# Seven block products instead of eight in both SwiGLUs of the last layer of a two-layer hybrid transformer

## The chip, the core and the metric

The kernel runs on one core of a Trainium2 chip. The core has a matrix engine (TensorE, "PE" in the rows, with its weight loads as "PEld"), a vector engine (DVE), an activation engine (ScalarE, "ACT"), GpSimd ("POOL") and a sync engine (SyncE, "SP") that issues the loads. Each engine runs its own instructions in order and waits on semaphores for the others. What counts is the device time of one execution, in microseconds (us).

## What is computed

Two layers work on 512 latent tokens and 256 context tokens of width 1024. Each layer is a SwiGLU half-step, a mixing block and a second SwiGLU half-step. The part that matters:

```python
def swiglu(x, w1, w3, w2):
    return (jax.nn.silu(x @ w1) * (x @ w3)) @ w2

def macaron_half(h, m, i, g, w1, w3, w2):
    y = swiglu(modulate(rms_norm(h, g), m[:, 3 * i], m[:, 3 * i + 1]), w1, w3, w2)
    return h + 0.5 * m[:, 3 * i + 2, None, :] * y
```

The hidden width is 2816. In the last layer the first SwiGLU runs on both streams (768 columns), the second on the latent tokens alone (512 columns).

## The kernel before

Activations lie transposed: 8 tiles `h[k]` of 128 features by 768 tokens, context in columns 0 to 255 and latents in 256 to 767. The normed input n exists as a high part `nhi` and a low part `nlo`, whose sum is the float32 value. Every product is three matmuls in `mm3` (L395 high by high, L396 high weight by low input, L397 low weight by high input). Weights are loaded in blocks of 128 by 1024 (`unit`, L387) into one of 3 `raw` buffers and split into one of 4 `w` tiles: ACT rounds to the high part (L402) and DVE subtracts it (L403).

`ffn` walks over 22 tiles f of 128 hidden features. `st1(f)` multiplies by w1 and w3: per weight 8 input tiles k, three matmuls each, on the 512 latent columns and on the 256 context columns, into the two big PSUM tiles S of two banks each. `evac` makes the gated value: silu on ACT (L638), the product on DVE (L639), its high part on ACT (L640), its low part on DVE (L641). Per pair of tiles `st2` multiplies by w2: 8 output tiles d, two f each, into one of 4 one-bank PSUM tiles B; DVE adds the result to h (L682). I call these the down products, or downs.

The first pair of tiles is made while the norm before it still delivers its operands. The norm (`norm_steps`) takes 1/rms from PSUM ("R") and then makes each tile: DVE scales h (`nt`, L594), ACT rounds it to `nhi` (L596), DVE subtracts for `nlo` (L599). One tile of a narrow norm goes to GpSimd. In the first SwiGLU of the last layer the latent columns come first and the context's after them; in the second the latents come in two halves of 256.

A list scheduler puts the instructions of each engine in order ahead of time, by the order of the program and by a model of the engines; what is said below of order is what it gave.

## Time and profile before

| | us |
|---|---|
| median of 3 runs | 2809.39 (2806.04 to 2809.98) |
| span of the profiled execution | 2808.0 |
| TensorE busy in it | 2741.3 (98%) |
| DVE busy | 1705.1 (61%) |
| ACT busy | 884.7 (32%) |
| last layer, first SwiGLU (768 columns) | about 1557 to 2122 |
| last layer, second SwiGLU (512 columns) | about 2431 to 2808 |

The profile is one execution. "Busy" of PE counts a matmul from its start to its modelled end, and neighbours overlap, so the duration of a matmul in a row (0.28 us for 256 columns) is longer than the distance from one start to the next (0.12 us). All costs of matmuls here are such distances. On DVE and ACT too the next instruction can start a little before the one ahead is done. The granted clock is the share of its full speed that TensorE was given.

### The profile page before, as it was taken

The page shows a single profiled execution, that of the slowest core. Times are in us where ns is not written, and L with a number is a line of the kernel's source. Part 1 is how long each engine was busy: PE and PEld are TensorE (multiplying, and loading weights), DVE is VectorE, ACT ScalarE, POOL GpSimd, SP SyncE. Part 2 cuts the span into 40 slices and gives each one's busy share as a digit, 9 for nine tenths or more (in the row PEclk, how much of TensorE's full clock was granted, in tenths as well). Part 3 has the DMA queues.
Part 4 walks back from the last instruction along what each step waited for, and adds up shares of the span by engine and source line. Part 5 has one row for each costly group of instructions (what it writes and reads, how often), then busy time and mean ns, then how long its engine had stood idle before and what let it go on. Part 6 is the DMA issues. An engine that isn't in the chain of part 4 may idle for free.

```text
span 2808.0 us, 38620 instructions
## 1 busy us (share of the span) xinstructions
PE 2741.3 (98%) x15548; PEld 2331.5 (83%) x15548; DVE 1705.1 (61%) x3071; ACT 884.7 (32%) x1553; POOL 287.3 (10%) x378
## 2 busy tenths in 40 slices
PE   6999999999899999999999999999999899999999
PEld 5788888889777788888888888888888777888887
DVE  8987767564875479986744644343446775454444
ACT  5311112133665441211211512112115665432221
POOL 5000000020442200000000200000001442100000
PEclk9999999999999999999999999999999999999999
DMA  6533334111200054454411212212111200133222
GB/s 227 173 122 128 129 104 141 63 57 55 79 1 16 19 173 143 164 166 130 156 60 61 64 58 68 68 46 76 61 60 53 77 22 23 39 113 96 92 98 75
DMA packets 78663, 249.50 MB, mean 89 GB/s; under 512 B 8978, under 2 KB 10642, under 8 KB 78484
## 3 DMA queue, kind: packets, MB, share of 16 engines
q1 hardware_dynamic: 78484, 247.03, 26.9%
q8 instruction: 122, 2.00, 0.3%
q14 instruction: 57, 0.47, 0.1%
HBM read 244.90 MB, written 2.10 MB: 88 GB/s over the span
## 4 chain that ended last, share of the span: by engine, by line
PE 91%; DVE 5%; ACT 2%; POOL 1%; issue 1%; DMA 0%; SPq 0%; DVEq 0%; ACTq 0%; POOLq 0%
PE S L396 17%; PE S L395 17%; PE S L397 17%; PE B L395 11%; PE B L396 11%; PE B L397 11%; PE B L1151 3%; PE B L1302 2%; PE B L1270 1%; DVE junk L482 1%; DVE w L403 0%; DVE nt L274 0%; PE B L543 0%; PE B L1195 0%; ACT P L1139 0%
## 5 line engine op out<-in xcount | busy, mean ns | idle before, releaser
L396 PE MATMUL S<-nlo,w 128*128 128x512 f32 (+1 forms) x2448 | 847.8, 347 | 6.6 <-DVE nlo L276 5.2
L395 PE MATMUL S<-nhi,w 128*128 128x512 f32 (+1 forms) x2448 | 837.7, 346 | 7.1 <-ACT nhi L596 3.0
L397 PE MATMUL S<-nhi,w 128*128 128x512 f32 (+1 forms) x2448 | 843.5, 345 | 0.0
L402 ACT CAST w<-raw 128x1024 fp32r<-128x1024 f32 (+1 forms) x309 | 317.6, 1042 | 1178.9 <-issue 858.2
L682 DVE SCALAR_TENSOR_TENSOR h<-B,g,h 128x512 f32<-128x512 f32 (+1 forms) x616 | 376.4, 634 | 323.4 <-PE B L397 322.8
L396 PEld LDWEIGHTS S<-nlo,w 128*128 128x128 f32 x2448 | 462.0, 189 | 69.6 <-DVE nlo L276 7.4
L395 PEld LDWEIGHTS S<-nhi,w 128*128 128x128 f32 x2448 | 459.7, 189 | 67.9 <-ACT nhi L596 3.6
L397 PEld LDWEIGHTS S<-nhi,w 128*128 128x128 f32 x2448 | 462.3, 189 | 58.5
L403 DVE TENSOR_TENSOR w<-raw,w 128x1024 fp32r<-128x1024 f32 (+1 forms) x309 | 375.4, 1227 | 222.0 <-ACT w L402 219.8
L395 PE MATMUL B<-ghi,w 128*128 128x512 f32 (+1 forms) x1232 | 426.5, 348 | 0.0
L396 PE MATMUL B<-glo,w 128*128 128x512 f32 (+1 forms) x1232 | 425.9, 346 | 0.0
L397 PE MATMUL B<-ghi,w 128*128 128x512 f32 (+1 forms) x1232 | 425.1, 346 | 0.0
L482 DVE CUSTOM_DVE_ANT_0 junk<-ada,bc,mpart 128x768 f32<-128x768 f32 x238 | 244.5, 1027 | 41.6 <-DMA ada<-in_w_ada 36.4
L396 PEld LDWEIGHTS B<-glo,w 128*128 128x128 f32 x1232 | 232.4, 189 | 35.4 <-issue 1.3
L395 PEld LDWEIGHTS B<-ghi,w 128*128 128x128 f32 x1232 | 231.8, 189 | 35.9 <-DVE h L682 1.3
L397 PEld LDWEIGHTS B<-ghi,w 128*128 128x128 f32 x1232 | 232.3, 189 | 31.1
L639 DVE TENSOR_TENSOR silu<-silu,S 128x768 f32<-128x768 f32 (+2 forms) x89 | 75.3, 846 | 235.5 <-PE S L397 225.2
L531 POOL TENSOR_TENSOR sq<-sq,sq 128x512 f32<-128x512 f32 (+1 forms) x38 | 44.3, 1165 | 1642.0 <-ACT sq L527 1640.9
L638 ACT ACTIVATE silu<-S 128x768 f32<-128x768 f32 (+2 forms) x89 | 64.5, 725 | 316.4 <-PE S L397 315.8
L482 DVE CUSTOM_DVE_ANT_0 junk<-ada,bc,sml 128x256 f32<-128x256 f32 x238 | 119.2, 501 | 4.2
L1145 POOL TENSOR_SCALAR P<-P,rd 128x768 f32<-128x768 f32 (+3 forms) x120 | 97.6, 816 | 216.8 <-DVE rd L1144 203.2
L1134 DVE TENSOR_REDUCE nm<-S 128x1 f32<-128x768 f32 (+3 forms) x120 | 94.6, 792 | 37.6 <-PE S L397 28.9
(227 smaller groups left out, 3152.4 us busy)
## 6 DMA issues: line engine op xcount, KB each, us to landing
raw<-in_w SPq DMA_DIRECT2D x264, 512.0 KB, 3.6
ada<-in_w_ada SPq DMA_DIRECT2D x171, 384.0 KB, 4.1
raw<-in_w_out SPq DMA_DIRECT2D x16, 512.0 KB, 3.8
ada<-in_ada SPq DMA_DIRECT2D x16, 384.0 KB, 6.1
raw<-in_w_in_t SPq DMA_DIRECT2D x10, 512.0 KB, 3.3
raw<-in_dftx SPq DMA_DIRECT2D x8, 512.0 KB, 3.3
ada<-in_ada SPq DMA_DIRECT2D x8, 256.0 KB, 7.1
h<-in_hT SPq DMA_DIRECT2D x8, 256.0 KB, 5.8
```

Source lines behind the costliest of these rows:

```text
L395: mm(out, lhs[0], rhs[0], start=start, stop=False)
L396: mm(out, lhs[0], rhs[1], start=False, stop=False)
L397: mm(out, lhs[1], rhs[0], start=False, stop=stop)
L402: nc.scalar.copy(hi, src)
L403: nc.vector.tensor_sub(lo, src, hi.bitcast(F32))
L482: nc.vector.tensor_tensor_reduce(out=self.junk[:, 0:w.shape[1]], in0=w, in1=v, scale=1.0, scalar=init, op0=ALU.mult, op1=ALU.add, accum_ou ...
L638: self.last_silu = nc.scalar.activation(s, p1, AF.Silu)
L639: nc.vector.tensor_mul(s, s, p3)
L682: nc.vector.scalar_tensor_tensor(out=self.h[d][:, c0:c1], in0=ps[:, 0:c1 - c0], scalar=gate()[:, d, s:s + 1], in1=self.h[d][:, c0:c1], op0 ...
L1134: self.last_max = nc.vector.tensor_reduce(out=nm, in_=ps[:, c0:c1], axis=AX.X, op=ALU.max, negate=True)
L1145: nc.gpsimd.tensor_scalar(out=P, in0=P, scalar1=rd, scalar2=1.0, op0=ALU.mult, op1=ALU.mult)
L1151: mm(outs[y], lhs[y], rhs[y], start=start, stop=stop)
```

## The change

In the last layer `ffn7` takes the place of `ffn`. The input n is cut into two halves of its features (tiles 0 to 3 and 4 to 7) and two halves of its columns (`n1` and `n2`: 384 wide in the first SwiGLU, 256 in the second); the weights of a pair of f tiles are cut likewise, into four blocks of 512 inputs by one f tile of w1 and of w3. The first pair is made as before, in eight block products (`first_pair`). Each of the other 10 pairs is made in seven products, in the order B11, B21, E, t3, t1, t4, B22. A product is 2 by 4 by 3 matmuls, 24 in all, into one S tile, and the tiles keep running sums: before the next product is added, ACT copies the tile to SBUF (`snapshot`, 3 per pair), and a later result is PSUM plus a copy (`gated`: DVE adds, ACT takes silu, DVE multiplies; L883 to L885 of the new kernel).

The products need sums of weight blocks, 4 per pair on DVE (L967 to L971, 128 by 1024 each), so that 7 blocks are split per pair instead of 4, with w2's 2 as before. They need sums of the four quarters of n, made once per SwiGLU (`combine`, L834 to L837, 16 instructions) and split into 8 more operand pairs `cu` and `cv`. For that the norm ahead keeps its float32 tiles (`nf` instead of `nt`), finishes each in place on ACT (L610), and sends no tile to GpSimd. `raw` buffers go from 3 to 5, the 3 KB slots from 46 to 44. The downs of a pair follow B11 of the next one in the program. The rotary tables of the last layer are made after its first SwiGLU. The weights of w1 and w3 of the last layer are packed by blocks. The lines of the code behind the diff's first edits stand one or more lower in the new kernel (L403 becomes L404, L594 becomes L600, L599 becomes L605).

```diff
-    def __init__(self, b, l, shift, goff, ns, n=None):
+    def __init__(self, b, l, shift, goff, ns, n=None, keep=False):
         self.b, self.l, self.shift, self.goff, self.ns, self.n = b, l, shift, goff, ns, n
         self.acc, self.a = {}, None
+        self.t = {} if keep else None
-        pool = () if cols[1] - cols[0] == SEQ else (5,)
-        return self.b.norm_steps(self.acc, cols, self.n, self.l, self.shift, self.a, pool)
+        pool = () if cols[1] - cols[0] == SEQ or self.t is not None else (5,)
+        return self.b.norm_steps(self.acc, cols, self.n, self.l, self.shift, self.a, pool, self.t)
...
-    def __init__(self, nc, tc, aps, pools, slots=46, wslots=4, raws=3):
+    def __init__(self, nc, tc, aps, pools, slots=44, wslots=4, raws=5):
...
-            ts[k] = self.m3(w, base="nt")
+            if keep is None:
+                ts[k] = self.m3(w, base="nt")
+            else:
+                if k not in keep:
+                    keep[k] = self.m3(base="nf")
+                ts[k] = keep[k][:, c0:c1]
             nc.vector.scalar_tensor_tensor(out=ts[k], in0=self.h[k][:, c0:c1], scalar=a(k)[:, s:s + 1], in1=box["R"][:, 0:w],
                                            op0=ALU.mult, op1=ALU.mult)
             nc.scalar.activation(n[k][0][:, c0:c1], ts[k], AF.Identity, bias=shift(k))
...
         def rest(k):
             done[k] = nc.vector.scalar_tensor_tensor(out=n[k][1][:, c0:c1], in0=ts[k], scalar=shift(k),
                                                      in1=n[k][0][:, c0:c1].bitcast(F32), op0=ALU.add, op1=ALU.subtract)
-            self.free(ts.pop(k))
+            if keep is None:
+                self.free(ts.pop(k))
+            else:
+                nc.scalar.activation(ts[k], ts[k], AF.Identity, bias=shift(k))
...
+    def block(self, src):
+        r = self.mp.tile([128, 1024], F32, tag="raw", name=self.name("raw"), bufs=self.raws)
+        if src is not None:
+            self.nc.sync.dma_start(r, src)
+        return r
+    def split_block(self, r, scale=None):
+        w = self.mp.tile([128, 2, 1024], F32R, tag="w", name=self.name("w"), bufs=self.wslots)
+        self.split_psum(w[:, 0], w[:, 1], r, scale)
+        return w
...
+    def ffn7(self, l, i, n, t, gate, nxt, streams=(X_COLS, C_COLS), split=None, late=None):
...
+        mp13, w2 = self.a["w13s"][i], self.a["w2"][l, i]
+        x_only = len(streams) == 1
+        halves = X_HALVES if x_only else ((0, T // 2), (T // 2, T))
+        wd = halves[0][1] - halves[0][0]
+        n1, n2 = (slice(*c) for c in halves)
+        off = {X_COLS: 512, C_COLS: 256}
+        np_ = NF // 2
...
+        def combine(k):
+            u, v = t.pop(k), t.pop(k + 4)
+            tensor = nc.vector.tensor_tensor
+            tensor(out=u[:, n1], in0=u[:, n1], in1=u[:, n2], op=ALU.subtract)
+            tensor(out=u[:, n2], in0=v[:, n2], in1=u[:, n2], op=ALU.subtract)
+            tensor(out=v[:, n2], in0=u[:, n1], in1=v[:, n2], op=ALU.add)
+            tensor(out=v[:, n1], in0=v[:, n2], in1=v[:, n1], op=ALU.subtract)
+            c = slice(halves[0][0], halves[1][1])
+            for x, name in ((u, "u"), (v, "v")):
+                hi, lo = self.hl(T, "c" + name)
+                self.split_psum(hi[:, c], lo[:, c], x[:, c])
+                tt[k, name] = hi, lo
+            self.free(u, v)
...
+        def product(bank, w, name, start):
+            for x in range(2):
+                for k in range(4):
+                    self.mm3(bank[:, x * 512:x * 512 + wd], [w[:, p, x * 512 + k * 128:x * 512 + k * 128 + 128] for p in range(2)],
+                             operand(name, k), start and k == 0, k == 3, not start)
...
+        def snapshot(bank, base):
+            y = self.m3(2 * wd, base=base)
+            v = y.rearrange("p (x c) -> p x c", x=2)
+            nc.scalar.copy(v, both(bank))
+            return y, v
...
+        def gated(s, cols, bank, y, sign):
+            z = self.m3(2 * wd, base="z")
+            zv = z.rearrange("p (x c) -> p x c", x=2)
+            nc.vector.tensor_tensor(out=zv, in0=both(bank), in1=y[1], op=ALU.add)
+            self.last_silu = nc.scalar.activation(s[:, cols], zv[:, 0], AF.Silu, scale=sign)
+            nc.vector.scalar_tensor_tensor(out=s[:, cols], in0=zv[:, 1], scalar=sign, in1=s[:, cols], op0=ALU.mult, op1=ALU.mult)
+            self.free(z)
...
+        def first_pair():
+            ws = {(m, q): self.split_block(self.block(mp13[0, m, q])) for m in range(2) for q in range(2)}
...
+                pc = [view(px[0], C_COLS), view(px[1], C_COLS), *(self.psB()[:, 0:CTX] for _ in range(2))]
+                for m in range(2):
+                    for x in range(2):
+                        for k in range(8):
+                            mm1(pc[2 * m + x], m, x, k, C_COLS)
...
+        def pair(j, middle):
+            fs = (2 * j, 2 * j + 1)
+            src = mp13[j]
+            add = nc.vector.tensor_add
+            Y, X = (self.ps("S", (j + x) % 2) for x in range(2))
+            r11 = self.block(src[0, 0])
+            product(Y, self.split_block(r11), "B11", True)
+            middle()
+            y0 = snapshot(Y, "y")
+            gtiles(j)
+            s = [self.m3(base="silu") for _ in range(2)]
+            r12 = self.block(src[0, 1])
+            product(X, self.split_block(r12), "B21", True)
+            r21, r22, s1 = self.block(src[1, 0]), self.block(src[1, 1]), self.block(None)
+            gated(s[0], n1, X, y0, 1.0)
+            self.free(y0[0])
+            parts(fs[0], s[0], n1)
+            add(s1, r21, r22)
+            add(r21, r11, r21)
+            add(r11, s1, r11)
+            product(Y, self.split_block(r11, -1.0), "E", False)
+            add(r12, r11, r12)
+            y1 = snapshot(Y, "y")
+            product(X, self.split_block(r21), "t3", True)
+            w0 = snapshot(X, "y")
+            product(Y, self.split_block(s1), "t1", False)
+            done_with(j, "u")
+            gated(s[1], n2, Y, w0, -1.0)
+            self.free(w0[0])
+            product(X, self.split_block(r22), "t4", False)
+            done_with(j, "v")
+            gated(s[1], n1, X, y1, -1.0)
+            self.free(y1[0])
+            parts(fs[1], s[1], slice(halves[0][0], halves[1][1]))
+            product(Y, self.split_block(r12), "B22", False)
+            self.last_silu = nc.scalar.activation(s[0][:, n2], Y[:, 0:wd], AF.Silu)
+            nc.vector.tensor_mul(s[0][:, n2], s[0][:, n2], Y[:, 512:512 + wd])
+            parts(fs[0], s[0], n2)
+            self.free(s)
+        self.table(AF.Silu, self.norm_sqrt)
+        first_pair()
+        for k in range(4):
+            combine(k)
...
+        def middle(j):
+            def go():
+                ws, fs = second(j), (2 * j, 2 * j + 1)
+                for d in range(8):
+                    for cols in streams:
+                        down(fs, ws, d, cols)
+                self.free([g.pop(f) for f in fs])
+            return go
+        for j in range(1, np_ - 1):
+            pair(j, middle(j - 1))
+        fs = (NF - 2, NF - 1)
+        if x_only:
+            pair(np_ - 1, middle(np_ - 2))
+        else:
+            held = {}
+            def go():
+                held["ws"], held["fs"] = second(np_ - 2), (NF - 4, NF - 3)
+                for d in range(8):
+                    down(held["fs"], held["ws"], d, X_COLS)
+            pair(np_ - 1, go)
+            for d in range(8):
+                down(held["fs"], held["ws"], d, C_COLS)
+            self.free([g.pop(f) for f in held["fs"]])
+        ws = second(np_ - 1)
+        for d in range(8):
+            down(fs, ws, d, X_COLS)
+            nxt.tile(d, X_COLS)
+        if late:
+            late()
+        if not x_only:
+            steps = nxt.steps(X_COLS)
+            steps.pop(0)()
+            self.table(AF.Sqrt, self.last_silu)
+            for d in range(8):
+                down(fs, ws, d, C_COLS)
+                nxt.tile(d, C_COLS)
+                if steps:
+                    steps.pop(0)()
+            for step in steps + nxt.steps(C_COLS):
+                step()
...
             if l:
-                with self.later(2000):
-                    tabs = self.rope_tables(l)
-            self.ffn(l, 0, n, self.gate(l, 2, 2, 0.5), nxt, begin=None if l else begin, mods=2)
+                tabs = []
+                self.ffn7(l, 0, n, t, self.gate(l, 2, 2, 0.5), nxt, late=lambda: tabs.extend(self.rope_tables(l)))
+            else:
+                self.ffn(l, 0, n, self.gate(l, 2, 2, 0.5), nxt, begin=begin, mods=2)
...
-            nxt = Next(self, l, 6, SM_GF2, ns)
+            nxt = Next(self, l, 6, SM_GF2, ns, keep=last)
...
-                self.ffn(l, 1, n, self.gate(l, 8, 2, 0.5), Next(self, l + 1, 0, SM_GF1, 2, n), mods=3)
+                nxt = Next(self, l + 1, 0, SM_GF1, 2, n, keep=True)
+                self.ffn(l, 1, n, self.gate(l, 8, 2, 0.5), nxt, mods=3)
+                t = nxt.t
-                self.ffn(l, 1, n, self.gate(l, 8, 1, 0.5), Done(self), streams=(X_COLS,), split=X_HALVES)
+                self.ffn7(l, 1, n, nxt.t, self.gate(l, 8, 1, 0.5), Done(self), streams=(X_COLS,), split=X_HALVES)
```

Three places show how the order moves. The first is DVE in the first SwiGLU of the last layer, during the norm of the context columns (`nt`, `nf`: scaled h; `nlo`: low part of an operand; `silu`, `glo`: gated value and its low part of the first pair). Before:

```order
L599 SCALAR_TENSOR_TENSOR nlo_9180<-nt_14124,mT,nhi_9179 128x256
L594 SCALAR_TENSOR_TENSOR nt_14131<-h_71,a_13910,B_14114 128x256
L599 SCALAR_TENSOR_TENSOR nlo_9182<-nt_14127,mT,nhi_9181 128x256
L594 SCALAR_TENSOR_TENSOR nt_14135<-h_72,a_13910,B_14114 128x256
L639 TENSOR_TENSOR silu_14295<-silu_14295,B_14189 128x512
L599 SCALAR_TENSOR_TENSOR nlo_9184<-nt_14131,mT,nhi_9183 128x256
L594 SCALAR_TENSOR_TENSOR nt_14139<-h_73,a_13910,B_14114 128x256
```

After, at the same tiles:

```order
L918 TENSOR_TENSOR glo_14185<-silu_14287,ghi_14184 128x512
L834 TENSOR_TENSOR nf_13995<-nf_13995 128x384
L605 SCALAR_TENSOR_TENSOR nlo_9184<-nf_14003,mT,nhi_9183 128x256
L600 SCALAR_TENSOR_TENSOR nf_14035<-h_73,a_13910,B_14122 128x256
L834 TENSOR_TENSOR nf_13998<-nf_13998 128x384
L605 SCALAR_TENSOR_TENSOR nlo_9186<-nf_14019,mT,nhi_9185 128x256
L600 SCALAR_TENSOR_TENSOR nf_14051<-h_74,a_13910,B_14122 128x256
L835 TENSOR_TENSOR nf_13995<-nf_14035,nf_13995 128x384
L834 TENSOR_TENSOR nf_14003<-nf_14003 128x384
L835 TENSOR_TENSOR nf_13998<-nf_14051,nf_13998 128x384
L605 SCALAR_TENSOR_TENSOR nlo_9188<-nf_14035,mT,nhi_9187 128x256
```

The sums of `combine` have moved in between the low parts of the context's operands.

The second is DVE in a steady pair of the second SwiGLU (`w<-raw`: low part of a weight block; `z`: PSUM plus a copy). Before:

```order
L403 TENSOR_TENSOR w_23197<-raw_23195,w_23197 128x1024
L639 TENSOR_TENSOR silu_23123<-silu_23123,S_23072 128x512
L403 TENSOR_TENSOR w_23202<-raw_23200,w_23202 128x1024
L641 TENSOR_TENSOR glo_23122<-silu_23123,ghi_23121 128x512
L403 TENSOR_TENSOR w_23271<-raw_23269,w_23271 128x1024
L639 TENSOR_TENSOR silu_23190<-silu_23190,S_23139 128x512
```

After, from the split of the second w2 block (`w_24243`) to the split of block E (L407):

```order
L404 TENSOR_TENSOR w_24243<-raw_24241,w_24243 128x1024
L885 SCALAR_TENSOR_TENSOR silu_24007<-z_24168,silu_24007 128x256
L967 TENSOR_TENSOR raw_24351<-raw_24347,raw_24349 128x1024
L986 TENSOR_TENSOR silu_24006<-silu_24006,S_23895 128x256
L968 TENSOR_TENSOR raw_24347<-raw_24207,raw_24347 128x1024
L404 TENSOR_TENSOR w_24320<-raw_24318,w_24320 128x1024
L858 TENSOR_TENSOR glo_24005<-silu_24007,ghi_24004 128x512
L858 TENSOR_TENSOR glo_24003<-silu_24006,ghi_24002 128x256
L969 TENSOR_TENSOR raw_24207<-raw_24351,raw_24207 128x1024
L971 TENSOR_TENSOR raw_24318<-raw_24207,raw_24318 128x1024
L883 TENSOR_TENSOR z_24352<-S_24206,y_24310 128x512
L407 SCALAR_TENSOR_TENSOR w_24361<-raw_24207,w_24361 128x1024
```

Two block sums (L967, which waits for the load `raw_24349`, and L968) now stand ahead of the low part of block B21 (`w_24320`).

The third is TensorE at the end of the kernel, from the last products into S to the last pair's downs (B). Before:

```order
L396 MATMUL S_23904<-nlo_21444,w_23900 128x512
L397 MATMUL S_23904<-nhi_21443,w_23900 128x512
L395 MATMUL S_23904<-nhi_21445,w_23900 128x512
L396 MATMUL S_23904<-nlo_21446,w_23900 128x512
L397 MATMUL S_23904<-nhi_21445,w_23900 128x512
L395 MATMUL B_23970<-ghi_23812,w_23962 128x512
L396 MATMUL B_23970<-glo_23813,w_23962 128x512
L397 MATMUL B_23970<-ghi_23812,w_23962 128x512
```

After:

```order
L396 MATMUL S_24825<-nhi_21552,w_25104 128x256
L397 MATMUL S_24825<-nlo_21553,w_25104 128x256
L398 MATMUL S_24825<-nhi_21552,w_25104 128x256
L396 MATMUL B_25145<-ghi_24932,w_25137 128x512
L396 MATMUL B_25154<-ghi_24932,w_25137 128x512
L396 MATMUL B_25163<-ghi_24932,w_25137 128x512
L396 MATMUL B_25172<-ghi_24932,w_25137 128x512
L397 MATMUL B_25145<-glo_24933,w_25137 128x512
L398 MATMUL B_25145<-ghi_24932,w_25137 128x512
```

Before, the downs began with the tile f made one step earlier; now they begin with `ghi_24932`, which the last product (into `S_24825`) gives.

## Rows read from the trace of the kernel before

**Rows 1.** The profile page: the engines' busy time, share of the span and instructions.
```profile
PE 2741.3 (98%) x15548; PEld 2331.5 (83%) x15548; DVE 1705.1 (61%) x3071; ACT 884.7 (32%) x1553; POOL 287.3 (10%) x378
```

**Rows 2.** The chain that ended last, shares of the span by engine.
```profile
PE 91%; DVE 5%; ACT 2%; POOL 1%; issue 1%; DMA 0%; SPq 0%; DVEq 0%; ACTq 0%; POOLq 0%
```

**Rows 3.** Busy time by window: us, PE, PEld, DVE, ACT, POOL, clock, DMA.
```profile
1680.00:1740.00 60.00, 60.00 (x344) 52.39 (x343) 24.30 (x34) 9.10 (x10) 0.00 (x0) 1.00 0.16 53
2600.00:2660.00 60.00, 60.00 (x260) 48.59 (x259) 28.83 (x34) 13.96 (x17) 0.00 (x0) 1.00 0.30 97
```

**Rows 4.** Timeline of PE, first SwiGLU: start, us, engine, line, operation.
```profile
1701.64 0.40 PE L395 MATMUL S<-nhi,w 128*128 128x512 f32 x1
...
1707.22 0.28 PE L395 MATMUL S<-nhi,w 128*128 128x256 f32 x1
...
1710.08 0.40 PE L395 MATMUL S<-nhi,w 128*128 128x512 f32 x1
```

**Rows 5.** Timeline of PE in the first layer's mixing, matmuls of 384 columns.
```profile
729.14 0.34 PE L395 MATMUL B<-w,phi 128*128 128x384 f32 x1
...
730.88 0.33 PE L396 MATMUL B<-w,phi 128*128 128x384 f32 x1
```

**Rows 6.** Groups by line and shape, whole span: count, busy us, mean ns.
```profile
L403 DVE TENSOR_TENSOR w<-raw,w 128x1024 fp32r<-128x1024 f32 x303 | 369.7, 1232 | 204.2 <-ACT w L402 202.0 <-PE B L397 0.3
L402 ACT CAST w<-raw 128x1024 fp32r<-128x1024 f32 x303 | 312.6, 1046 | 1174.4 <-issue 858.2 <-PE S L397 216.2 <-PE B L397 93.0
L641 DVE TENSOR_TENSOR glo<-silu,ghi 128x768 fp32r<-128x768 f32 x58 | 55.2, 951 | 0.0
```

**Rows 7.** Timeline of DVE, neighbours without a wait (x2 joins two).
```profile
2606.64 0.68 DVE L641 TENSOR_TENSOR glo<-silu,ghi 128x512 fp32r<-128x512 f32 x1
2607.24 1.40 DVE L682 SCALAR_TENSOR_TENSOR h<-B,g,h 128x512 f32<-128x512 f32 x2
...
2617.60 2.35 DVE L403 TENSOR_TENSOR w<-raw,w 128x1024 fp32r<-128x1024 f32 x2
```

**Rows 8.** Timeline of DVE in the context norm of the first SwiGLU, first and last.
```profile
1586.22 0.87 DVE L594 SCALAR_TENSOR_TENSOR nt<-h,a,B 128x256 f32<-128x256 f32 x2 [1.13 <-ACT Rs L582]
1587.28 0.49 DVE L599 SCALAR_TENSOR_TENSOR nlo<-nt,mT,nhi 128x256 fp32r<-128x256 f32 x1 [0.19 <-ACT nhi L596]
...
1593.86 0.48 DVE L599 SCALAR_TENSOR_TENSOR nlo<-nt,mT,nhi 128x256 fp32r<-128x256 f32 x1
```

**Rows 9.** Timeline of DVE at the second SwiGLU's norm, a sum and its successor.
```profile
2429.69 0.42 DVE L531 TENSOR_TENSOR sq<-sq,sq 128x256 f32<-128x256 f32 x1
2430.03 0.48 DVE L1336 SCALAR_TENSOR_TENSOR h<-B,g,h 128x256 f32<-128x256 f32 x1
```

**Rows 10.** Busy time by window at the entry of the second SwiGLU.
```profile
2428.90:2431.40 2.50, 0.02 (x1) 0.00 (x0) 2.50 (x6) 2.44 (x5) 1.01 (x2) 1.00 0.56 162
2431.40:2438.40 7.00, 6.64 (x29) 6.35 (x30) 6.27 (x15) 3.24 (x7) 0.83 (x1) 0.51 0.26 92
```

**Rows 11.** DMA issues in the second SwiGLU: count, KB each, median us to landing.
```profile
raw<-in_w SPq DMA_DIRECT2D x41, 512.0 KB, 3.4
```

**Rows 12.** DMA issues in the first 60 us of the kernel.
```profile
ada<-in_ada SPq DMA_DIRECT2D x15, 384.0 KB, 6.2
```

**Rows 13.** Timeline of DVE at the exit of the first SwiGLU.
```profile
2115.75 0.75 DVE L682 SCALAR_TENSOR_TENSOR h<-B,g,h 128x512 f32<-128x512 f32 x1 [0.41 <-PE B L397]
...
2123.96 1.40 DVE L594 SCALAR_TENSOR_TENSOR nt<-h,a,B 128x512 f32<-128x512 f32 x2 [1.22 <-PE B L560]
```

**Rows 14.** Timeline of GpSimd at the exit of the first SwiGLU.
```profile
2108.80 2.67 POOL L531 TENSOR_TENSOR sq<-sq,sq 128x512 f32<-128x512 f32 x2 [519.76 <-ACT sq L527]
```

**Rows 15.** Timeline of DVE at the end of the kernel.
```profile
2792.97 0.69 DVE L639 TENSOR_TENSOR silu<-silu,S 128x512 f32<-128x512 f32 x1 [6.08 <-PE S L397]
2794.35 0.69 DVE L641 TENSOR_TENSOR glo<-silu,ghi 128x512 fp32r<-128x512 f32 x1 [0.69 <-ACT ghi L640]
...
2804.12 0.75 DVE L682 SCALAR_TENSOR_TENSOR h<-B,g,h 128x512 f32<-128x512 f32 x1 [0.65 <-PE B L397]
```

More of the change, by code (lines that the diff above doesn't have):

```diff
@@ L390, in unit, with mm3 @@
         return w
[L392 removed]
+    def mm3(self, out, lhs, rhs, start, stop, more=False):
         mm = self.nc.tensor.matmul
[L395 to L397 removed]
+        mm(out, lhs[0], rhs[0], start=start, stop=False, skip_group_check=more)
+        mm(out, lhs[0], rhs[1], start=False, stop=False, skip_group_check=more)
+        mm(out, lhs[1], rhs[0], start=False, stop=stop, skip_group_check=more)
     def split_psum(self, hi, lo, src, scale=None):
@@ L562, in rms_row, with norm_steps @@
         return R
[L564 removed]
+    def norm_steps(self, st, cols, n, l, mod, a, pool=(), keep=None):
         nc = self.nc
@@ L775, in ffn @@
                 st2(fs, ws, d, C_COLS)
+                nxt.tile(d, C_COLS)
[3 more added lines that the diff above has]
+                step()
+        for q in fs:
+            self.free(g.pop(q))
+    def block(self, src):
[7 more added lines that the diff above has]
+        return w
```

73 lines of the change are left out of this document (67 added, 6 removed).

## The prediction

> **What bounds the kernel now.** I read the busy times first, then the chain that ended last, then single stretches. TensorE is busy 98% of the span [rows 1] and carries 91% of the chain [rows 2]; DVE is busy 61%, ACT 32%. So TensorE's matmuls set the time, and fewer or shorter ones are worth their full length where the other engines can keep up. In the last layer's SwiGLUs they can today: over 60 us of either, TensorE has no idle time, DVE works 24 and 29 us, ACT 9 and 14 us, at full clock [rows 3]. The reader should see there how much room DVE has in a steady pair, since the change fills it. The steady stretches tell nothing of the two places where DVE, not TensorE, is short already: the norms at the entry of each SwiGLU [rows 8, 10].
>
> **What it removes.** One pair of f tiles before took, for w1 and w3, 96 matmuls of 512 columns (2 tiles by 2 weights by 8 by 3), and in the first SwiGLU 96 of 256 as well. Now it takes 7 times 24, or 168, of 384 columns (first SwiGLU) or 256 (second). The price of one is the distance between starts: 512 columns 60/260 = 0.2308 us [rows 3]; 256 columns (1710.08 - 1707.22)/24 = 0.1192 [rows 4]; 384 columns 1.74/10 = 0.174 [rows 5], and 0.175 halfway between the other two; I take 0.175. First SwiGLU: 96 x 0.350 = 33.6 before, 168 x 0.175 = 29.4 now, 4.2 saved, in 10 pairs 42. Second: 96 x 0.2308 = 22.16 before, 168 x 0.1192 = 20.03 now, 2.13 saved, 21.3 in all. Together **63.3 us**. The other price for 384 moves this by 2 us. The 256-wide price comes from runs of 24 between wider ones; that it holds over 31 us on end is an extension.
>
> **What it adds in a steady pair.** On DVE a queued instruction costs its duration less about 0.09: two block splits take 2.35, not 2 x 1.23, so 1.12 each; a 512-wide sum 0.60 (2606.64 to 2607.24), an addition to h 0.66 [rows 7]; 768 wide 0.86 [rows 6]; a 256-wide sum 0.34 [rows 9], a 256-wide norm step 0.39 [rows 8]; 384 wide, halfway, 0.47. A pair of the second SwiGLU gives DVE 9 splits and 4 block sums (13 x 1.12 = 14.6), 8 additions to h (5.3), and 4.6 for gating: 24.5 us. TensorE needs 20.0 + 48 x 0.2308 = 31.1. A pair of the first: 14.6 + 8.4 + 6.5 = 29.5 against 29.4 + 16.8 = 46.2. ACT has 9 casts of 1.05 less 0.1 [rows 6] and some 4 us of copies and silus: 12.6. By sums all of it is hidden.
>
> By order one place is tight, in the second SwiGLU only: block B21's low part. The load of the last block of the sums can start when DVE has split w2's first block, which frees its buffer. From there: load 3.4 [rows 11], block sum 1.12, gating product 0.34, block sum 1.12, low part 1.23, hand-overs 0.2: 7.4. TensorE has for that time the products B22 and the next B11 (48 x 0.1192 = 5.7), six matmuls that are ready (1.2), and starts 0.3 later: 7.2. I price 0.15 in each of 9 pairs, 1.4; the bounds are 0 and 8 (0.9 a pair, if the load lands 0.7 later). The copies of running sums cost nothing: 24 matmuls (2.9 us) of the other S tile lie between a product and the next one on the same tile, the copy takes about 0.6. In the first SwiGLU the same chain has over 10 us.
>
> **First pair of the first SwiGLU.** From the context's first `nt` to its last `nlo` DVE now has, in its order, 16 norm steps (6.3), 2 steps of the first pair's gating (1.2), 12 sums of `combine` (5.6), one weight split (1.1) and two splits of `cu` (1.7): 16.0 us, against 7.64 before (1586.22 to 1593.86) [rows 8]. TensorE can start 1.0 after the first `nt` and has 96 x 0.1192 = 11.4 to do; it ends at about 16.0 + 0.5 + 0.9 instead of 12.4, a wait of 5.0, in pieces. Then the first downs wait for w2's low part, which stands behind more splits (1.4), and the next product for the S tile, whose reading by DVE stands behind four splits and two sums (2.0). **8.4**. [...] These waits are shorter, so I take 2 (0 to 7): **10.4** (5 to 15.4).
>
> **First pair of the second SwiGLU.** From the second half's first `nt` to the product that frees the S tile for B11, DVE has 16 norm steps (6.3), 12 sums of 0.34 (4.1), 2 weight splits (2.2), 3 splits of `cu`, `cv` (1.8) and the product itself (0.7): 15.1. TensorE is through with that half after 1.0 + 11.4 = 12.4 and a little waiting, so it waits about 3; then 0.7 for `ghi` of the first down and 0.9 for block E, whose sums stand behind the last splits: 5. A wait of 3 us is like that of [rows 10], so another 3.4 for the clock. The norm itself has 8 tiles on DVE instead of 7 and 8 more ACT steps per half: 1.5. **9.9** (5 to 15).
>
> [...]
>
> **Exit and tail.** At the exit of the first SwiGLU the chain from the last addition to h to the first scaled tile of the next norm is 8.2 us (2115.75 to 2123.96), and about 1.5 more to the first product on it [rows 13]. Before, the context's last w1 and w3 products and its downs covered it; now only its downs (48 x 0.1192 = 5.7) and the norm's own matmuls (some 3): 1.5 with the clock (0 to 5). The rotary tables now stand in GpSimd's queue ahead of that norm's sums, and wait for slots that the last products free; GpSimd stood idle 520 us before these sums [rows 14], so I price them at nothing (up to 2 if a slot comes late). At the very end the last pair's downs began with the older f tile while the gating ran (2.07 us from product to `glo`, 512 wide [rows 15]); now they begin with the tile that the last product completes: silu, product, cast at 256 columns, some 0.42 each and hand-overs, 1.6. With the clock 3 (1.6 to 5).
>
> **Sum.** -63.3 + 10.4 + 9.9 + 1.4 + 1.5 + 3 = -37.1. Made against the span of 2808.0, that is 2770.9; the median shown is 1.4 above the span, so **2772 us**. With every loss at its lower end (5 + 5 + 0 + 0 + 1.6 = 11.6) it would be 2758, at its upper one (15.4 + 15 + 8 + 5 + 5 = 48.4) 2794.5.
>
> **Rivals.** (A) *Nothing new waits.* If the semaphores let DVE's sums pass in TensorE's shadow after all, only the tail's 1.6 stays: 2809.4 - 63.3 + 1.6 = 2748. For it: DVE has a fifth or more of its time to spare in each steady pair. Against it: the order at both entries is fixed, and there DVE's queue is longer than TensorE's work. (B) *Each pair of the second SwiGLU waits for its loads, and the time ends above the one before.* Of a pair's 6 loads three go out within 5 us, when buffers come free in a row, and the third is the one in the tight chain. In the crowded first 60 us of the kernel a load takes 6.2 us to land [rows 12], 2.8 more than in [rows 11]; B21 then waits 2.9 in each of 9 pairs, as long as the wait of [rows 10], so each is followed by some 3.4 of lost clock: 6.2 x 9 = 56, 2828 us. It decides from 37/9 = 4.1 us a pair, that is from a load about 2 us later if the clock falls each time. Against it: 41 loads landed in 3.4, with the DMA engines busy 0.30 of the time [rows 3, 11]. [...] (C) *The second SwiGLU's products bring nothing, or every pair of both loses 1 to 1.5 us without the clock falling.* Were 256-wide matmuls 0.132 us apart (22.16/168), 21.3 are gone: 2793; 19 pairs at 1.0 to 1.4 give 2791 to 2799. Against it: 0.1192 at full clock [rows 4]. That the change does not do what it says is excluded: TensorE has 15275 instead of 14796 instructions in order, as 10 x (168 - 192) + 10 x (168 - 96) asks, but for one.
>
> **How the numbers follow.** My sum, 2755 to 2788: 0.62. A, below 2755: 0.12. C, 2785 to 2803: 0.13. B, above that: 0.13, most of it over 2815. The range 2748 to 2800 leaves out B and a part of A and C, under 0.2 together. About 0.2% (5.6 us) is what a measurement of this kernel can tell from no change. Faster by more: A, my sum and nearly all of C, 0.85. Within 0.2%: what is left of C and the lower edge of B, 0.04. Slower: 0.11.
>
> **What the profile would show.** Starts of 256-wide matmuls 0.119 apart and of 384-wide 0.175 in the steady pairs; a pair's period 46.2 and 31.2 us, with DVE busy some 29 and 25 of it. Idle time of TensorE of about 8 us in the first SwiGLU's first pair, released by `nlo` and low parts of weights on DVE, and 3 before the second's first B11, released by the gating product, with a granted clock near 0.5 behind it; a gap of 1.6 before the last downs. I am wrong if steady pairs show a gap before the third matmul of B21 of over 1 us (B), if DVE's gating or sums take longer than the rows used here, or if no clock falls at the entries (then 8 us less).

## The result and the profile after

The changed kernel took 2759.81 us (median of 4 runs, 2758.63 to 2764.89) beside 2809.68 for the one before: 0.9833 of it, with a 95% interval of 0.9819 to 0.9848. It is 50 us faster; 37 had been forecast. A second set of runs of it, told of below, gave 0.9827.

The page of the changed kernel, busy times and the shares of the chain that ended last, answers to [rows 1] and [rows 2]. TensorE still sets the time; VectorE (DVE) rose from 61% to 70%.

```profile
PE 2681.3 (97%) x16028; PEld 2346.5 (85%) x16028; DVE 1937.3 (70%) x3385; ACT 1015.0 (37%) x1773; POOL 280.6 (10%) x372
...
PE 88%; DVE 6%; ACT 2%; issue 2%; DMA 1%; POOL 1%; SPq 0%; DVEq 0%; ACTq 0%; POOLq 0%
```

To see where the time went I cut both spans at an instruction that both kernels have once per norm, the matmul that spreads 1/rms over the partitions (L560 before, L561 after). Here it is in TensorE's timeline (start, us, engine, line, operation), in the kernel before:

```profile
1560.17 1.02 PE L560 MATMUL B<-diag,ones 128*128 128x512 f32 x2
...
2122.01 1.91 PE L560 MATMUL B<-diag,ones 128*128 128x512 f32 x2
...
2426.49 0.59 PE L560 MATMUL B<-diag,ones 128*128 128x256 f32 x2
```

and in the changed one:

```profile
1562.74 1.02 PE L561 MATMUL B<-diag,ones 128*128 128x512 f32 x2
...
2092.53 1.02 PE L561 MATMUL B<-diag,ones 128*128 128x512 f32 x2
...
2393.31 0.59 PE L561 MATMUL B<-diag,ones 128*128 128x256 f32 x2
```

The last matmul begins at 2803.68 before and at 2753.49 after. So, in us:

| stage | before | after | difference | forecast |
|---|---|---|---|---|
| up to the norm of the last layer's first SwiGLU | 1560.17 | 1562.74 | +2.6 | 0 |
| first SwiGLU, up to the next norm | 561.84 | 529.79 | -32.1 | -30.1 |
| mixing, up to the next norm | 304.48 | 300.78 | -3.7 | 0 |
| second SwiGLU, up to the last matmul | 377.19 | 360.18 | -17.0 | -7.0 |
| sum | 2803.68 | 2753.49 | -50.2 | -37.1 |

One thing moves with the cut. Of the context's downs (256 columns wide, 0.119 us each) 30 stand behind the cut after the first SwiGLU in the kernel before and 12 in the changed one, which is 2.1 us. By work, then, the first SwiGLU is 34.2 us shorter and the mixing 1.6.

The steady pairs did nearly as forecast. These two windows of the changed kernel (us, then busy time of PE, PEld, DVE, ACT, POOL, granted clock, DMA) answer to [rows 3]: nearly all of the ten pairs of the first SwiGLU, and 285 us inside the second.

```profile
1613.28:2074.19 460.91, 460.90 (x2628) 439.94 (x2628) 311.12 (x393) 150.01 (x192) 4.93 (x8) 1.00 0.21 69
2450.00:2735.00 285.00, 284.62 (x1970) 262.15 (x1969) 230.78 (x281) 120.01 (x173) 0.00 (x0) 1.00 0.31 100
```

The length of a pair is read from the first down of one pair to that of a later pair. Here are eight pairs of the second SwiGLU on TensorE, in the kernel before:

```profile
2503.40 0.39 PE L395 MATMUL B<-ghi,w 128*128 128x512 f32 x1
...
2770.39 0.39 PE L395 MATMUL B<-ghi,w 128*128 128x512 f32 x1
```

and in the changed one:

```profile
2461.75 1.10 PE L396 MATMUL B<-ghi,w 128*128 128x512 f32 x4
2462.85 0.39 PE L398 MATMUL S<-nhi,w 128*128 128x256 f32 x1
2463.07 0.28 PE L396 MATMUL S<-nhi,w 128*128 128x256 f32 x1
...
2712.62 1.10 PE L396 MATMUL B<-ghi,w 128*128 128x512 f32 x4
```

A pair of the second took 266.99/8 = 33.37 us before and takes 250.87/8 = 31.36 now (31.1 to 31.25 forecast). A pair of the first, read in the same way, took 404.51/8 = 50.56 before (1667.96 to 2072.47) and takes 231.66/5 = 46.33 now (1749.72 to 1981.38; 46.2 forecast). DVE works 25.4 us of a pair of the second (24.5 forecast) and 31.3 of one of the first (29.5). TensorE's idle time in the 285 us is 0.4.

The rows also show the tight place, which idle time hides because the ends of neighbours overlap. L398 at 2462.85 is the third matmul of B21. It starts 1.10 us after the first of the four matmuls ahead of it, where four distances of 0.2308 make 0.92, and the next one 0.22 after it, where 0.12 is usual.

What TensorE waits for lies at the entries and the tail. This is its idle time at the context norm and the first pair of the first SwiGLU (1590 to 1616), summed by line and by the instruction that ended it (total us, times, longest); it makes 6.0 us:

```profile
PE S L397 <- DVE nlo L605: 2.6, 5, 0.9
PE S L396 <- DVE silu L915: 1.4, 1, 1.4
PE S L396 <- ACT nhi L602: 0.9, 1, 0.9
PE B L398 <- DVE w L404: 0.8, 1, 0.8
PE B L396 <- ACT w L403: 0.3, 1, 0.3
```

And this is the longest of it from the second SwiGLU's norm to the end:

```profile
PE S L396 <- DVE silu L915: 2.5, 1, 2.5
PE B L396 <- ACT ghi L857: 1.4, 1, 1.4
PE S L396 <- ACT nhi L602: 1.1, 1, 1.1
PE S L396 <- ACT w L406: 0.9, 1, 0.9
PE S L397 <- DVE nlo L605: 0.8, 2, 0.6
```

The entry and the tail have the waits that were forecast, by the engines that were named: 2.5 for the gating product on DVE, 0.9 for block E, 1.4 for the last `ghi`. What differs is the clock behind them. The kernel before ran at 0.51 for 7 us after its wait [rows 10]; the changed one at 1.00 after as long a wait:

```profile
2425.27:2428.97 3.70, 3.70 (x28) 3.57 (x29) 3.70 (x7) 2.86 (x6) 0.00 (x0) 1.00 0.02 4
```

### The profile page after: what moved, and what is told of

It is laid out like the page before. It is cut to its first block, busy times and chain, and to the rows that moved or that the text cites. A ratio compares the mean times of both kernels' runs of the same rounds, so it can differ in the third digit from the quotient of the medians.

```text
span 2757.9 us, 40164 instructions
## 1 busy us (share of the span) xinstructions
PE 2681.3 (97%) x16028; PEld 2346.5 (85%) x16028; DVE 1937.3 (70%) x3385; ACT 1015.0 (37%) x1773; POOL 280.6 (10%) x372
## 4 chain that ended last, share of the span: by engine, by line
PE 88%; DVE 6%; ACT 2%; issue 2%; DMA 1%; POOL 1%; SPq 0%; DVEq 0%; ACTq 0%; POOLq 0%
PE S L398 16%; PE S L396 16%; PE S L397 16%; PE B L396 11%; PE B L398 11%; PE B L397 11%; PE B L1409 3%; PE B L1560 2%; DVE w L404 1%; PE B L1528 1%; DVE junk L483 1%; ACT P L1397 0%; PE B L1453 0%; ACT w L403 0%; DMA ada<-in_w_ada 0%
## 5 line engine op out<-in xcount | busy, mean ns | idle before, releaser
L403 ACT CAST w<-raw 128x1024 fp32r<-128x1024 f32 x349 | 359.6, 1043 | 961.6 <-issue 539.0
L397 PE MATMUL S<-nlo,w 128*128 128x256 f32 (+2 forms) x1968 | 653.9, 333 | 7.0 <-DVE nlo L605 4.0
L398 PE MATMUL S<-nhi,w 128*128 128x256 f32 (+2 forms) x1968 | 652.5, 332 | 1.8 <-DVE w L404 1.7
L396 PE MATMUL S<-nhi,w 128*128 128x256 f32 (+2 forms) x1968 | 644.3, 333 | 9.1 <-DVE silu L915 3.9
L404 DVE TENSOR_TENSOR w<-raw,w 128x1024 fp32r<-128x1024 f32 x349 | 424.0, 1227 | 119.3 <-ACT w L403 117.1
L398 PE MATMUL B<-ghi,w 128*128 128x512 f32 (+1 forms) x1232 | 425.1, 346 | 0.8 <-DVE w L404 0.8
L397 PEld LDWEIGHTS S<-nlo,w 128*128 128x128 f32 x1968 | 371.9, 189 | 44.3 <-DVE nlo L605 7.5
L396 PEld LDWEIGHTS S<-nhi,w 128*128 128x128 f32 x1968 | 369.1, 189 | 45.0 <-DVE silu L915 4.5
L398 PEld LDWEIGHTS S<-nhi,w 128*128 128x128 f32 x1968 | 372.0, 189 | 38.8 <-DVE w L404 6.4
L398 PEld LDWEIGHTS B<-ghi,w 128*128 128x128 f32 x1232 | 231.9, 188 | 31.2 <-DVE w L404 1.0
L1397 ACT ACTIVATE P<-S,nm 128x768 f32<-128x768 f32 (+3 forms) x120 | 93.0, 776 | 56.0 <-DVE nm L1392 31.6
```

Of the source, the lines that this page charges most:

```text
L396: mm(out, lhs[0], rhs[0], start=start, stop=False, skip_group_check=more)
L397: mm(out, lhs[0], rhs[1], start=False, stop=False, skip_group_check=more)
L398: mm(out, lhs[1], rhs[0], start=False, stop=stop, skip_group_check=more)
L403: nc.scalar.copy(hi, src)
L404: nc.vector.tensor_sub(lo, src, hi.bitcast(F32))
L1397: self.last_exp = nc.scalar.activation(P, ps[:, c0:c1], AF.Exp, bias=nm, scale=1.0, accum_out=den)
```

## The experiments

**One SwiGLU at a time.** Do the gains of the two SwiGLUs stand alone? The first kernel is the changed one with

```
-                self.ffn7(l, 1, n, nxt.t, self.gate(l, 8, 1, 0.5), Done(self), streams=(X_COLS,), split=X_HALVES)
+                self.ffn(l, 1, n, self.gate(l, 8, 1, 0.5), Done(self), streams=(X_COLS,), split=X_HALVES)
```

and `keep` left out of the norm ahead; the second has `ffn` in the first SwiGLU in the same way, with the rotary tables made where they were before.

> Of the change only the first SwiGLU's seven products are kept; the second SwiGLU is multiplied in eight as before, and its norm again gives one tile to GpSimd. In the changed kernel the first SwiGLU's stretch (1562.74 to 2092.53) was 32 us shorter than before's and the stretch behind it 3.7 shorter. Theory (the two SwiGLUs' gains add up): 32 to 36 us less than before, 2774 to 2778, and the second SwiGLU's stretch as long as before's 377.2. Rival (part of the gain is given back at the exit to the attention when the second part is absent): under 28 us less, over 2782.

> Of the change only the second SwiGLU's seven products are kept, with the norm ahead of it without a GpSimd tile; the first SwiGLU is multiplied in eight. My prediction's terms for the second SwiGLU gave 21.3 less 9.9, 1.4 and 3, so 7 us; the changed kernel's trace shows 377.19 to 360.18, so 17. Theory (the trace's 17 belong to this part alone): 17 to 20 us less than before, 2790 to 2793. Rival (some of it comes from the first SwiGLU's part, through buffers or order): near 7, 2803.

Measured: 2777.93 us, 0.9901 [0.9883, 0.9918], 28 us less than before; and 2796.97, 0.9971 [0.9959, 0.9984], 9 us less. Both miss the theory, and together they are worth 37 us where the whole is worth 47 (0.0167 x 2806). In the traces each SwiGLU keeps its own gain (first SwiGLU 530.51 us in the one, second 360.00 in the other). But in the second kernel the first SwiGLU, multiplied in eight as before, took 564.31 instead of 561.84, and all before it 1563.13 instead of 1560.17. Something of the change that both kernels share costs time in places that it does not speak of.

**The buffers.** The only edit that both share ahead of the last layer is `slots=46, raws=3` to `slots=44, raws=5`. Two kernels are the one before with that line, and with half of it:

```
-    def __init__(self, nc, tc, aps, pools, slots=46, wslots=4, raws=3):
+    def __init__(self, nc, tc, aps, pools, slots=44, wslots=4, raws=5):
```

```
+    def __init__(self, nc, tc, aps, pools, slots=44, wslots=4, raws=3):
```

> The kernel before, with five buffers for w1 and w3 blocks in place of three and two slots fewer, as the changed kernel has them. Theory (these buffers are worth nothing to eight products, whose loads are never late): 2808 to 2811, the wait of 2.53 us at the entry of the second SwiGLU as before. Rival (they shorten that entry): 2804 to 2805.

> The kernel before with two slots fewer (44), the number of load buffers for w1 and w3 left at three. With 44 slots and five load buffers it was 1.0032 [1.0019, 1.0045] of before, with a wait of 2.9 us at the first SwiGLU's context norm that before hasn't. Theory (five load buffers let the splits of weights be scheduled ahead of the norm): 1.000 here, no such wait. Rival (the two slots are what is missed): 1.003.

Measured: 2816.08 us, 1.0032 [1.0019, 1.0045], and 2816.09, 1.0038 [1.0023, 1.0053]. So the two slots cost about 10 us, and the load buffers nothing that can be told; both of my theories were wrong here. This price would also account for the sum above: each of the two kernels pays it, the changed kernel once, so the two gains together fall short of the whole by 10. That is an inference; the changed kernel with 46 slots was not run. The trace of the second shows one of the places, the context norm of the first SwiGLU on TensorE:

```profile
1593.24 0.59 PE L560 MATMUL B<-diag,ones 128*128 128x256 f32 x2
1593.48 0.58 PE L397 MATMUL B<-nhi,w 128*128 128x512 f32 x1
1596.95 0.51 PE L395 MATMUL S<-nhi,w 128*128 128x256 f32 x2 [2.89 <-ACT nhi L596]
```

and these are its windows behind that wait:

```profile
1596.95:1603.00 6.05, 5.99 (x35) 5.78 (x36) 5.14 (x13) 2.89 (x6) 0.35 (x1) 0.72 0.00 0
```

In the kernel before, the same norm matmul has 15 matmuls of 512 columns in the rows behind it, which cover the norm:

```profile
1585.12 0.59 PE L560 MATMUL B<-diag,ones 128*128 128x256 f32 x2
1585.36 0.58 PE L395 MATMUL B<-nhi,w 128*128 128x512 f32 x1
...
1588.81 0.40 PE L397 MATMUL B<-nhi,w 128*128 128x512 f32 x1
1589.05 0.40 PE L395 MATMUL S<-nhi,w 128*128 128x256 f32 x2
```

With two slots fewer TensorE's order has only one such matmul left behind it: a wait of 2.89 us, and the clock at 0.72 over the next 6. That stage is 3.6 us longer (565.43), in both kernels with 44 slots alike. The changed kernel has this order too (L561 at 1590.08, one such matmul, then a wait of 0.89 for `nhi`). The traces with three and with five load buffers put 4.6 and 3.5 us more in front of the last layer. In all kernels of this study that part runs the same program but for the slots and load buffers: with 46 slots it took 1560.2 and 1560.7, with 44 between 1559.7 and 1565.5, 1562.5 on average. That share is small beside its scatter. Over the whole span the two traces are 7.4 and 6.3 us longer than the one of before; where the rest of the 10 lies they don't show. Why the order comes out so is not settled; that it is the slots is shown.

**The GpSimd tile.** The kernel before, with the norm's sixth tile on DVE ahead of the second SwiGLU, as in the changed one:

```
-        pool = () if cols[1] - cols[0] == SEQ else (5,)
+        pool = () if cols[1] - cols[0] == SEQ or (self.l, self.shift) == (DEPTH - 1, 6) else (5,)
```

> The kernel before, with the one tile of the last layer's norm ahead of the second SwiGLU that GpSimd and ScalarE had made given to VectorE. Theory (the GpSimd tile's ScalarE operations, not the buffers, kept the first split of that norm from ScalarE, so that TensorE waited 2.53 us at 2431.45 and then ran at half clock to 2438.4): the wait is under 1 us, the clock doesn't fall, about 5 us less than before, 2804 to 2805. Rival 1 (the number of load buffers did it): no change, 2809 to 2810. Rival 2 (my prediction's price: eight tiles on VectorE are 1.5 us later): 2811.

Measured: 2807.56 us, 1.0004 [0.9995, 1.0014]. In the trace the theory's mechanism is there: the wait of 2.53 us is gone and the longest one near it is 0.64, the clock stays up (1.00 over the 7 us from 2430.4), and the stage to the end takes 374.28 us instead of 377.19.

```profile
2430.40:2437.40 7.00, 6.58 (x53) 6.39 (x54) 6.89 (x16) 3.50 (x8) 0.00 (x0) 1.00 0.48 150
```

One wait of 1.18 us, for `nhi` of the second half, is new. But the time did not move, and the interval leaves room for a gain of 1.4 us at most. The old entry's wait and fall are not an accident of one profile: the three other profiles with that entry (the kernel with only the first SwiGLU changed and the two of the buffers) have both, with a granted clock of 0.53 to 0.76 over the 7 us behind the wait and 376.5 to 378.1 us for the stage. So where the 2.9 us of the trace went in the time stays open. My price of 1.5 us for eight tiles on DVE has no support in the trace; the interval, up to 3.9 us slower, doesn't exclude it.

**The sums on GpSimd.** If DVE's 16 sums hold TensorE up at the entries, another engine could make them; and the last downs could begin with the tile that is ready.

```
-            tensor = nc.vector.tensor_tensor
+            tensor = nc.gpsimd.tensor_tensor
```

```
         ws = second(np_ - 1)
+        if x_only:
+            fs, ws = fs[::-1], ws[::-1]
```

> The changed kernel once more, unaltered, beside the runs of before of this chip. Expected: 0.983 of before, about 2758 where before is 2806. Its profile tells whether the wait of 2.53 us at the first product of the second SwiGLU's second half stays at the full clock, as at 2425.27 in the first profile of it, or is followed by half clock, as the same wait was in the kernel with only the second SwiGLU changed (0.58 over 2462.3 to 2466). Theory (the fall is a matter of chance from run to run): either may show, worth 2 us. Rival (it depends on the program): full clock again.

> The changed kernel with the 16 sums of norm tiles ahead of each of its SwiGLUs (the operands t1, t3, t4 and E) made by GpSimd, not VectorE. Theory (in the first pair TensorE waits for VectorE, which is behind by these sums, 16 times 0.34 to 0.5 us): the waits of 6.0 us in the first SwiGLU's first pair fall to about 2, those of 2.53 and 0.94 in the second's to 0.5, so about 6 us less than the changed kernel, 0.998 of it. Rival (GpSimd is slower at a sum than VectorE, and the splits of the sums, which stay on VectorE, come later still): the same waits or longer, 0 to 5 us more.

> The changed kernel with the last pair's products with w2 beginning with the gate tile that was ready first, not with the one made last. Theory: the wait of 1.37 us at 2742.45 for ScalarE's ghi goes and nothing takes its place, 1.4 us less than the changed kernel. Rival (the other tile's parts are wanted 8 products later and are late then): 0.

> Both of the last two edits. Theory: their gains add up, about 7 us less than the changed kernel. Rival: GpSimd's sums give nothing, so 1 us less or up to 4 more.

Measured: the changed kernel 2759.65 us, 0.9827 [0.9812, 0.9842]; GpSimd 2765.68, 0.9849 [0.9835, 0.9864]; the tail's order 2759.15, 0.9826 [0.9810, 0.9843]; both 2764.00, 0.9841 [0.9827, 0.9856]. The wait at the tail is gone (the second SwiGLU takes 359.23 us instead of 360.98 in the changed kernel's profile beside it); as time that is too little to tell. GpSimd made it worse by 6 us (by 4 with the tail's order), where the theories had 6 and 7 less, and in a way that I had not foreseen. Its timeline, and DVE's beside it:

```profile
1597.19 2.37 POOL L834 TENSOR_TENSOR nf<-nf 128x384 f32<-128x384 f32 x2
...
1598.60 0.47 DVE L600 SCALAR_TENSOR_TENSOR nf<-h,a,B 128x256 f32<-128x256 f32 x1
...
1603.47 1.76 DVE L404 TENSOR_TENSOR culo<-nf,cuhi 128x768 fp32r<-128x768 f32 x1
...
1605.15 1.23 DVE L605 SCALAR_TENSOR_TENSOR nlo<-nf,mT,nhi 128x256 fp32r<-128x256 f32 x1
```

The same operations with the sums on DVE, in the changed kernel:

```profile
1598.59 0.47 DVE L600 SCALAR_TENSOR_TENSOR nf<-h,a,B 128x256 f32<-128x256 f32 x1
1598.98 0.55 DVE L834 TENSOR_TENSOR nf<-nf 128x384 f32<-128x384 f32 x1
...
1599.92 0.47 DVE L605 SCALAR_TENSOR_TENSOR nlo<-nf,mT,nhi 128x256 fp32r<-128x256 f32 x1
...
1602.78 0.94 DVE L404 TENSOR_TENSOR culo<-nf,cuhi 128x768 fp32r<-128x768 f32 x1
```

Two sums take GpSimd 2.35 to 3.74 us in this stretch, 1.2 to 1.9 each, instead of 0.55. While it works, DVE's own splits stretch, in these rows from 0.94 to 1.76 and from 0.47 to 1.23; the norm step L600, which takes one operand from PSUM, keeps its 0.47. So the sums left DVE and DVE was no earlier. GpSimd's time varies as well: one weight split of DVE kept its 1.21 us (L404 at 1601.20) while two of GpSimd's sums took 3.74 together instead of 2.37.

**The sums left out, and held back.** Two more kernels ask what the sums cost. One leaves out the four sums of `combine`, so that its output is not the reference's; the other has the tail's order and

```
-        for k in range(4):
-            combine(k)
+        with self.tc.issue_after((self.last_mul if x_only else self.norm_last).ins):
+            for k in range(4):
+                combine(k)
```

> The changed kernel without the 16 sums of norm tiles in each of its SwiGLUs: the operands t1, t3, t4 and E are the norm's tiles themselves, so the output isn't the reference's, and every split, load and product stays. It measures what these 32 sums cost on VectorE. Theory (TensorE's waits in the first pair are VectorE's lateness, to which the sums add 16 times 0.47 us in the first SwiGLU and 16 times 0.34 in the second): the waits of 6.0 us in the first SwiGLU's first pair fall to 2 to 3, those of 2.53 and 0.94 us in the second's to 1 to 1.5 together, about 5 us less than the changed kernel. Rival (the waits are the chain norm, split, first product, whatever VectorE does beside it): within 1 us of the changed kernel.

> The changed kernel with the last pair's order of the run before (gate tile that was ready first) and with the 16 sums held back: in the first SwiGLU until the norm's last tile is split, in the second until the first pair's last product of silu and w3 is made. Theory (the sums stand ahead of nlo and silu on VectorE though nothing needs them until the third product of the next pair): 2 to 4 us less than the changed kernel, 2756. Rival (VectorE has no slack until that third product, so what is put off there comes back as a wait later): 0 to 3 us more.

Measured: without the sums 2755.82 us, 0.9819 [0.9803, 0.9835]; held back 2756.00, 0.9829 [0.9814, 0.9844], both beside 2805.94 for before. By their ratios neither can be told from the changed kernel (0.9827 and 0.9833), so what follows is read from the traces. Without the sums the first pair of the first SwiGLU has one wait of over half a us (0.89 for `nhi`), the 6.0 us of waits become 2.4, and that SwiGLU takes 526.59 us instead of 529.79; the 2.53 of the second becomes 0.77, the 0.94 is gone, and it takes 358.09 instead of 360.18. So the waits are DVE's lateness, to which the sums add; they are worth about 3 us at the first SwiGLU's entry and 2 at the second's. Holding them back gives the same 526.58 in the first SwiGLU. In the second it costs what it gave: the waits for the silu product and for block E go, and this one comes, on TensorE:

```profile
2432.28 0.50 PE L396 MATMUL B<-ghi,w 128*128 128x512 f32 x1 [3.19 <-DVE h L896]
```

Behind it the clock fell for 3.4 us (0.50), and that SwiGLU takes 361.28 us, 2 more than with the tail's order alone. There DVE has no slack to put anything off to; in the first SwiGLU it has. The last kernel takes that: held back in the first SwiGLU only, with the tail's order.

> The changed kernel with the last pair's order (gate tile that was ready first) and with the sums held back in the first SwiGLU alone, until the norm's last tile is split; the second SwiGLU's sums stay where the changed kernel has them. Theory (holding back gave 3.2 us in the first SwiGLU's trace, 529.8 to 526.6, and cost 2.1 in the second's, 359.2 to 361.3, and the tail's order gives 1.0 to 1.7): 4 to 5 us less than the changed kernel, first SwiGLU 526.6, second 359.2, ratio to before 0.9815. Rival (the gain of the first SwiGLU doesn't show in the time, as the whole did not in the run before): 0.983.

Measured: 2756.22 us, 0.9817 [0.9804, 0.9831]. Its second SwiGLU took 359.11 us, as the theory has it, its first 527.89, which is 1.3 more; there the clock was low at the start (256-wide matmuls 0.21 us apart instead of 0.12), until 1562.3. The median is 3.4 us under that of the changed kernel's second set (2759.65). The intervals overlap, so that it is the fastest is likely and not shown.

**The clock behind a wait.** Five profiles, of four kernels, have the same wait, 2.53 us for the silu product in the second SwiGLU. Three ran on at the full clock, 1.00 over the 3.7 us behind it (the changed kernel in both of its profiles, and the one with the tail's order). In two the clock fell within 1 us of the wait's end, to 0.58 over the same 3.7 us: the one with only the second SwiGLU changed and the last one. Here is the first of these two:

```profile
2462.31:2466.01 3.70, 3.70 (x19) 3.70 (x20) 3.70 (x7) 2.85 (x6) 0.00 (x0) 0.58 0.02 4
```

TensorE did 19 matmuls there instead of 28. In all five, TensorE's order is the same for over 100 us ahead of the wait, and from the norm's matmul (L561) to the wait's end its starts agree within 0.05 us. So that order does not decide it. The second profile of the changed kernel alone, at the full clock as its rival had it, would not have shown this.

The other profiles bear on the odds. In the eight-product kernels' entry to the second SwiGLU a wait of 2.53 us stands as well, in four profiles, and the clock fell in all four (0.51 to 0.76 over the 7 us behind it). The wait of 2.89 us in the kernel with 44 slots and three load buffers was met by a fall (0.72 over 6 us), so was the 3.19 us with the sums held back (0.50 for 3.4 us), and the tail's 1.37 us was not in five profiles (1.00 over the 4 us behind it). The clock also fell where there was no wait. At the norm ahead of the last layer's first SwiGLU eleven profiles have the same order on TensorE and no wait over 0.3 us in the 20 us before, and in six of them the clock fell. Here are the 5 us behind 1560 in the changed kernel and in the one with the tail's order:

```profile
1560.00:1565.00 5.00, 4.99 (x36) 4.30 (x37) 4.75 (x9) 2.01 (x6) 1.04 (x2) 1.00 0.33 105
```

```profile
1560.00:1565.00 5.00, 4.99 (x26) 4.05 (x25) 3.65 (x7) 1.67 (x5) 0.58 (x1) 0.67 0.32 105
```

Just before, from 1559.25 on, TensorE had done 16 matmuls of 2 columns in 1.7 us, at the same times within 0.03 us in both.

## Why the prediction was right, point by point

The sign, the mechanism and the range held; the time was 12 us lower than forecast. The total came out nearer than its terms did: costs that were put too high and one that was left out, the slots, went against each other.

- **What it removes, 63.3.** Right: ten pairs at 50.56 - 46.33 = 4.23 and ten at 33.37 - 31.36 = 2.01 make 62.4. The tight place's loss is already in that, so 63.3 - 1.4 = 61.9 is the forecast beside it. The 256-wide price held over 285 us; for 512 columns 0.232 is the distance between starts, against 0.2308 from the count in [rows 3].
- **The steady pair's tight place, 1.4.** Right in place and releaser, half the size. In each of nine pairs the third matmul of B21 starts 0.1 to 0.4 us late, and the next one 0.1: 0.3 a pair and 2.8 in all, within the bounds of 0 to 8. In six of the nine profiles with seven products in the second SwiGLU one pair waits 0.63 there.
- **First pair of the first SwiGLU, 10.4.** The waits were 6.0, not 8.4. The other 2 were set for the clock, as less than the 3.4 behind the longer wait of [rows 10]; no run shows this term, and here the granted clock was 1.00 from 1590 to 1616. The trace of the kernel without the sums confirms the mechanism.
- **First pair of the second SwiGLU, 9.9.** This step failed. Its waits were near: 0.6 + 0.2 + 1.1 + 2.5 + 0.2 + 0.9 + 0.3 = 5.8, forecast 5. But I set 3.4 for the clock (7.0 us at 0.51 in [rows 10] lose 7.0 x 0.49), which didn't fall (1.00 from 2393 to 2453), and 1.5 for the norm, whose second half began earlier, not later (15.9 us after the first half, 18.4 before). And I did not take off what the same place had cost before: a wait of 2.5 and the low clock behind it, which I had used as a price [rows 10] without seeing that the changed kernel would no longer have them. A count over the stage, from the two traces, gives the size. At 0.232 and 0.119 between starts its matmuls are 22.4 us shorter (1486 of 512 columns and 208 of 256 before, 527 and 1888 after). What starts later than that sums to 6.8 us before and 12.4 after, of which 1.6 lie at the tail, 2.8 in the tight place and 8.0 at the entry. So the entry cost 1.2 us more than the old one, not 9.9, and -22.4 + 5.6 = -16.8 is the table's -17.0 but for 0.2. The run without the GpSimd tile leaves open whether the time gains all of this.
- **Exit 1.5, tail 3.** Exit: 0.6 + 0.2 of waits. The mixing behind it is 1.6 shorter by work. The kernel before had a low clock there (0.50 from 2121.0 to 2124.3), and 3.3 us at half the clock lose 1.7 at most. The three kernels with eight products in the first SwiGLU and 44 slots had no fall there and took 302.7 to 303.5 us for this stage instead of 304.48. So the fall is the likely cause; no run isolates it. Tail: 1.4 of wait, as forecast (1.6); no clock (1.00 over the 4 us behind it).
- **What I had no term for.** The slots. I named 46 to 44 and priced it at nothing by leaving it out. In eight products they cost 10 us. The two kernels with one SwiGLU each speak for the changed kernel paying as much; its trace shows 2.6 ahead of the last layer, inside that part's scatter. If it does pay 10, then without them it would have come out near 2750, 22 below the forecast and 2 above the range's lower end, and it is luck that the forecast missed by only 12.
- **The rivals.** A (2748) is out: 6.0 + 5.8 + 1.4 = 13 us of waits are there. B, loads late in each pair with the clock falling, is out: no wait over 0.64 us in the steady pairs in any profile of seven products, and full clock over all 285 us. No load was as late as B has it, so no run shows what such a series of waits would do to the clock. C is out by the 256-wide starts.

Of the difference of 13 us between the forecast and the trace, 10 lie in the second SwiGLU, most of it at the entry, 4.1 in the first, 1.6 in the mixing behind it, and 2.6 the other way ahead of the last layer.

## What to carry to other kernels

When a stage is replaced, take off what its old entry cost, before adding what the new one will: the old entry's wait and its stretch at 0.51 were not kept here. A change of buffers is a change of every schedule that draws from them: two slots of 46 cost 10 us of 2806 in code that the change did not speak of, and one run with only that line changed shows it. A wait can be summed from rows; a clock fall behind it came in some profiles of one order and not in others (0.58 in two, 1.00 in three, behind the same 2.53 us), so it belongs in the range, with a chance, and not in the sum as a certain term.

## What the runs showed of the hardware

- The same order on TensorE with the same 2.53 us without a matmul was followed by a granted clock of 1.00 three times and of 0.58 twice, over 3.7 us. In another place, with no wait over 0.3 us in the 20 us before, the clock fell in six of eleven profiles of one order; over 5 us there it was 0.67 in one and 1.00 in another.
- With GpSimd summing float32 tiles in SBUF, two of DVE's splits, with operands in SBUF, took 1.9 and 2.6 times as long (0.94 to 1.76, 0.47 to 1.23), a weight split the same 1.21 and a norm step with a PSUM operand the same 0.47. A sum of 128 x 384 took GpSimd 1.2 to 1.9 us, DVE 0.55.
- In the changed kernel's steady pairs, matmuls of 384 columns began 0.176 us apart and of 256 columns 0.119 apart (medians), some 120 in a row, at full clock over 461 and 285 us.
